# A grouped 3x3 convolution: from two 64x128 TensorE tiles per tap to eight 32x64 tiles

## The chip, the cores and the metric

The kernel runs on one core of a Trainium2 chip. The metric is the device time of one execution in microseconds (us). Of the kernel before there are three runs: 154.03, 154.77 and 154.79 us, median 154.77 us. Lower is better.

## The reference

A 2-D convolution with a 3x3 kernel, padding 1 and 8 groups, on 16 images of 64x64 pixels. 64 input channels become 128 output channels; a group is 8 input channels and 16 output channels.

```python
batch, c_in, h, w, c_out, k, groups = 16, 64, 64, 64, 128, 3, 8
x_pad = np.pad(x, ((0, 0), (0, 0), (pad, pad), (pad, pad)), mode='constant')
# for each group g, image b, output channel co, input channel ci of the group, tap (kh, kw):
output[b, g * c_out_per_group + co] += \
    weight[g * c_out_per_group + co, ci, kh, kw] * \
    x_pad[b, g * c_in_per_group + ci, kh:kh+h, kw:kw+w]
```

x and the output are float32: 16.8 MB are read and 33.6 MB written. The arithmetic on TensorE is in bf16 with float32 sums.

## The kernel before

**Layout.** Two images of 64 channels fill the 128 partitions. An image lies in SBUF as one flat row of 4096 bf16 pixels per channel, with 66 zeros ahead of it and behind it (`PADL`, `PADR`). Eight such pairs make the batch (`NPAIR`). The loads are cast from float32 to bf16 on the way, and are issued from Pool's queue (lines 106 and 118); the first pair is loaded image by image into two buffers, `xpa` and `xpb`, so that its work can start early.

**Taps as shifts.** A tap (kh, kw) is a shift of the flat row by `W*(kh-1) + (kw-1)`. For each chunk of 512 pixels (8 rows) the loop at line 162 issues nine taps, each with two matmuls at line 170: one on the upper 64 rows of the array for the first image, one on the lower 64 rows for the second. Each has 64 input channels by all 128 output channels, with the weights of the other groups as zeros, and accumulates in a PSUM bank of its own (`pcs[h]`).

**Edges.** A flat shift runs over the ends of image rows: the taps with kw = 0 and kw = 2 add, in the first and last column, pixels of the neighbouring row. What they add too much is computed separately: VectorE gathers the two border columns into `xc` (lines 128 to 131), twelve small matmuls a pair (line 149) multiply them into `fxa` and `fxb`, and VectorE subtracts these from the output tile (lines 213 and 218).

**Copies and stores.** Each bank is copied to the output tile `ob` by ScalarE (line 195) or VectorE (line 197), in turns. Stores go out on Pool's queue (line 223), half an image at a time, in the last pair a quarter.

**Weights.** They are loaded on the sync queue (line 48, `w_sb`), transposed by a matmul with an identity (line 51), expanded to block form by nine float32 matmuls with selection matrices (line 84) and masked by VectorE into `wtap` (line 88). Pool builds the selection matrices and the mask with selects (lines 58, 72, 76).

**What sets the order.** The framework orders each engine's instructions by readiness and by their place in the program, and puts in the semaphores. Each engine's queue then runs in that order. Buffers: six for input, six for output, two PSUM banks for each of `pc0` and `pc1`.

Of the kernel before, what the change touches and what calls it, by code (L numbers as in the profile page):

```python
# [8 lines left out]
FP32 = mybir.dt.float32  # L10
BF16 = mybir.dt.bfloat16


@with_exitstack
def kernel(
# [7 lines left out]
    nc = tc.nc  # L23

    B, C, H, W = x.shape
    CO, CIg, K, _ = weight.shape
    G = groups
    COg = CO // G
    HW = H * W
    assert C == 64 and CO == 128 and K == 3 and B % 2 == 0  # L30

    PADL = W + 2
    PADR = W + 2
    XBUF = PADL + HW + PADR

    wpool = ctx.enter_context(tc.tile_pool(name="wpool", bufs=1))
    xpool = ctx.enter_context(tc.tile_pool(name="xpool", bufs=6))
    opool = ctx.enter_context(tc.tile_pool(name="opool", bufs=6))
    colpool = ctx.enter_context(tc.tile_pool(name="colpool", bufs=3))
    psum_o = ctx.enter_context(tc.tile_pool(name="psum_o", bufs=2, space=bass.MemoryType.PSUM))  # L40
    psum_f = ctx.enter_context(tc.tile_pool(name="psum_f", bufs=2, space=bass.MemoryType.PSUM))

    ident = wpool.tile([128, 128], FP32)
    make_identity(nc, ident)

    w_sb = wpool.tile([128, CIg * K * K], FP32)
    with tc.high_priority(offset=100000):
        nc.sync.dma_start(w_sb, weight.rearrange("co ci kh kw -> co (ci kh kw)"))

    wT_ps = psum_f.tile([128, 128], FP32, tag="fixA", name="wT_ps")  # L50
    nc.tensor.transpose(wT_ps[0 : CIg * K * K, :], w_sb, ident)  # L51
    wT = wpool.tile([128, 128], FP32)
    nc.vector.tensor_copy(wT[0 : CIg * K * K, :], wT_ps[0 : CIg * K * K, :])  # L53

    sel = wpool.tile([128, 9, 128], FP32)
    nc.vector.memset(sel, 0.0)
    for t in range(9):
        nc.gpsimd.affine_select(  # L58
            out=sel[:, t, :],
            in_=sel[:, t, :],  # L60
            compare_op=mybir.AluOpType.not_equal,
            fill=1.0,
            base=-t,
            channel_multiplier=1,
            pattern=[[0, 2], [0, G], [-9, CIg]],
        )

    maskBD = wpool.tile([128, 128], FP32)
    nc.vector.memset(maskBD, 0.0)
    for h in range(2):  # L70
        msl = maskBD[64 * h : 64 * h + 64, :]
        nc.gpsimd.affine_select(
            out=msl, in_=msl, compare_op=mybir.AluOpType.is_gt, fill=1.0,
            base=1 - CIg, channel_multiplier=1, pattern=[[-CIg, G], [0, COg]],
        )
        nc.gpsimd.affine_select(  # L76
            out=msl, in_=msl, compare_op=mybir.AluOpType.is_ge, fill=0.0,
            base=0, channel_multiplier=1, pattern=[[-CIg, G], [0, COg]],
        )

    wtap = wpool.tile([128, 9, 128], BF16)
    for t in range(9):
        U = psum_f.tile([128, 128], FP32, tag="fixA", name=f"U{t}")
        nc.tensor.matmul(  # L84
            U, lhsT=sel[0 : CIg * K * K, t, :], rhs=wT[0 : CIg * K * K, :],
            start=True, stop=True,
        )
        nc.vector.tensor_mul(wtap[:, t, :], U, maskBD)  # L88

    x_pairs = x.rearrange("b c h w -> (b c) (h w)").rearrange(  # L90
        "(i p) s -> i p s", p=128
    )
    out3 = out.rearrange("b co h w -> b co (h w)")

    NPAIR = B // 2
    NCHUNK = HW // 512
    xps = {}

    def emit_load(i):
        if i == 0:  # L100
            xpa = xpool.tile([128, XBUF], BF16, name="xpa", tag="xpa", bufs=1)
            xpb = xpool.tile([128, XBUF], BF16, name="xpb", tag="xpb", bufs=1)
            for h, t_ in enumerate((xpa, xpb)):
                nc.vector.memset(t_[64 * h : 64 * h + 64, 0:PADL], 0.0)
                nc.vector.memset(t_[64 * h : 64 * h + 64, PADL + HW :], 0.0)
                nc.gpsimd.dma_start(
                    t_[64 * h : 64 * h + 64, PADL : PADL + HW],
                    x_pairs[0][64 * h : 64 * h + 64, :],
                )
            xps[i] = (xpa, xpb)  # L110
            return
        xp = xpool.tile([128, XBUF], BF16, name="xp")
        nc.vector.memset(xp[:, 0:PADL], 0.0)
        nc.vector.memset(xp[:, PADL + HW :], 0.0)
        npiece = 2 if i == 1 else 1
        ppc = HW // npiece
        for pp in range(npiece):
            nc.gpsimd.dma_start(  # L118
                xp[:, PADL + ppc * pp : PADL + ppc * (pp + 1)],
                x_pairs[i][:, ppc * pp : ppc * (pp + 1)],  # L120
            )
        xps[i] = (xp, xp)

    emit_load(0)
    emit_load(1)

    def emit_gather(xp, xc):
        nc.vector.memset(xc, 0.0)
        xp3 = xp[:, PADL : PADL + HW].rearrange("p (h w) -> p h w", w=W)
        nc.vector.tensor_copy(xc[:, 2 : 2 + H], xp3[:, :, W - 1])  # L130
        nc.vector.tensor_copy(xc[:, 72 : 72 + H], xp3[:, :, 0])

    for i in range(NPAIR):
        if i + 2 < NPAIR:
            emit_load(i + 2)
        xph = xps.pop(i)

        fixs = [
            psum_f.tile([128, 2, H], FP32, tag="fixA", name="fxa"),
            psum_f.tile([128, 2, H], FP32, tag="fixB", name="fxb"),  # L140
        ]
        xc = colpool.tile([128, 152], BF16, name="xc")

        def emit_fix_group(g):
            h, e = g // 2, g % 2
            pr = 64 * h
            off = 0 if e == 0 else 72
            for kh in range(3):
                nc.tensor.matmul(  # L149
                    fixs[h][:, e, :],  # L150
                    wtap[pr : pr + 64, 3 * kh + 2 * e, :],
                    xc[pr : pr + 64, off + kh : off + kh + H],
                    start=(kh == 0), stop=(kh == 2), tile_position=(pr, 0),
                )

        fix_c0 = 3 if i < 2 else 0

        ob = [
            opool.tile([128, HW], FP32, name=f"ob{h}_{i}", tag="ob") for h in range(2)
        ]  # L160

        for c in range(NCHUNK):
            pcs = [psum_o.tile([128, 512], FP32, name=f"pc{h}") for h in range(2)]
            for t in range(9):
                kh, kw = t // 3, t % 3
                d = W * (kh - 1) + (kw - 1)
                base = PADL + 512 * c + d
                for h in range(2):
                    pr = 64 * h
                    nc.tensor.matmul(  # L170
                        pcs[h],
                        wtap[pr : pr + 64, t, :],
                        xph[h][pr : pr + 64, base : base + 512],
                        start=(t == 0), stop=(t == 8), tile_position=(pr, 0),
                    )
            if c == fix_c0:
                if i > 0:
                    emit_gather(xph[0], xc)
                else:
                    for h in range(2):  # L180
                        xp3 = xph[h][64 * h : 64 * h + 64, PADL : PADL + HW]
                        xp3 = xp3.rearrange("p (h w) -> p h w", w=W)
                        nc.vector.memset(xc[64 * h : 64 * h + 64, :], 0.0)
                        nc.vector.tensor_copy(  # L184
                            xc[64 * h : 64 * h + 64, 2 : 2 + H], xp3[:, :, W - 1]
                        )
                        nc.vector.tensor_copy(  # L187
                            xc[64 * h : 64 * h + 64, 72 : 72 + H], xp3[:, :, 0]
                        )
            if fix_c0 <= c < fix_c0 + 4:  # L190
                emit_fix_group(c - fix_c0)
            for h in range(2):
                dst = ob[h][:, 512 * c : 512 * (c + 1)]
                if (c + h) % 2 == 0:
                    nc.scalar.copy(dst, pcs[h])  # L195
                else:
                    nc.vector.tensor_copy(dst, pcs[h])  # L197

            if c == 0:
                stored = 0  # L200
            last_pair = i == NPAIR - 1
            qn = 4 if last_pair else 2
            qc = NCHUNK // qn
            if c >= fix_c0 + 3:
                ready_q = (c + 1) // qc
                while stored < ready_q:
                    q = stored
                    stored += 1
                    r0 = q * (H // qn)
                    s0 = r0 * W  # L210
# [51 lines left out]
```

## Time and profile before

| What | Value |
|---|---|
| median of the three runs | 154.77 us |
| span of the profiled execution, first to last instruction | 152.7 us |
| busy share: TensorE, its weight loads | 90%, 59% |
| busy share: VectorE, ScalarE, Pool | 41%, 25%, 20% |
| mean rate of the DMA | 276 GB/s |
| read from and written to HBM | 16.81 MB, 33.55 MB |

The span is that of one execution under the profiler; the run times are those of whole executions, so the median lies 2.1 us above the span. In the page, PE is TensorE's matmuls, PEld its weight loads, DVE VectorE, ACT ScalarE, POOL GpSimd and SP SyncE. Two rows cut the span into 40 slices of 3.8 us: one with the busy share in tenths, one with the rate in GB/s. The DMA's rate counts bytes where they land, so a load that is cast from float32 to bf16 counts with half of what it reads. In the groups of instructions, a row gives the line, engine, operation, operands, shapes and count, then busy us and mean ns of one, then the engine's idle time before them and what ended it.

### The profile page before, as it was taken

How to read it: one execution, taken by the hardware profiler on the slowest of the kernel's cores; microseconds unless marked ns; L12 is line 12 of the kernel's file. 1: busy time of each engine (PE TensorE's matmuls, PEld its weight loads, DVE VectorE, ACT ScalarE, POOL GpSimd, SP SyncE). 2: the span in 40 equal slices, each digit the busy share in tenths (PEclk: the TensorE clock that was granted, in tenths of full speed). 3: DMA queues.
4: the chain of work that ended last, by engine and by line, in shares of the span. 5: the costliest groups of instructions: out<-in, count | busy, mean ns of one | idle time of the engine just before them, and what ended most of it. 6: DMA issues, size and time to landing. Idle time of an engine off the chain costs nothing.

```text
span 152.7 us, 3024 instructions
## 1 busy us (share of the span) xinstructions
PE 137.4 (90%) x1267; PEld 90.7 (59%) x1267; DVE 62.0 (41%) x193; ACT 38.8 (25%) x65; POOL 29.8 (20%) x65
## 2 busy tenths in 40 slices
PE   1199999999999999999999999999999999999700
PEld 0155344577766667766776667766776677667400
DVE  6132153454334535353535353434353535454400
ACT  3000113322222333333333333222223333333300
POOL 7990000112011402020202020201101020214220
PEclk9999999999999999999999999999999999999965
DMA  3489999999999999999994929394948576696961
GB/s 63 84 149 207 228 210 219 217 213 219 159 419 427 419 404 210 369 416 434 423 416 208 414 107 412 137 378 178 369 180 339 217 309 245 275 406 260 374 276 63
DMA packets 6654, 42.18 MB, mean 276 GB/s; under 512 B 880, under 2 KB 880, under 8 KB 2160
## 3 DMA queue, kind: packets, MB, share of 16 engines
q0 software_dynamic: 6496, 41.95, 81.3%
q8 instruction: 10, 0.16, 0.4%
q1 hardware_dynamic: 144, 0.04, 0.1%
q14 instruction: 4, 0.03, 0.1%
HBM read 16.81 MB, written 33.55 MB: 330 GB/s over the span
## 4 chain that ended last, share of the span: by engine, by line
PE 89%; DMA 3%; issue 2%; POOL 0%; DVE 0%; POOLq 0%; DVEq 0%
PE pc L170 84%; PE U L84 4%; DMA xpa<-in_x_dram 3%; PE fxa L149 1%; PE fxb L149 1%; POOLq L257 0%; POOL out_dram L223 0%; DVE xc L187 0%; POOL ident masks.py:197 0%; DVE xc L184 0%; DVE wT L53 0%; POOLq L223 0%; POOLq masks.py:199 0%; DVEq L184 0%; POOLq L243 0%
## 5 line engine op out<-in xcount | busy, mean ns | idle before, releaser
L170 PE MATMUL pc<-xp,wtap 64*128 64x512 bf16 x1008 | 110.8, 376 | 0.0
L170 PEld LDWEIGHTS <-wtap 64*128 64x128 bf16 x1152 | 85.2, 94 | 38.0 <-issue 3.7
L197 DVE COPY ob<-pc 128x512 f32<-128x512 f32 x64 | 44.3, 692 | 72.1 <-PE pc L170 72.1
L195 ACT COPY ob<-pc 128x512 f32<-128x512 f32 x64 | 37.5, 586 | 105.2 <-PE pc L170 104.1
L223 POOL DMA_DIRECT2D out_dram<-ob x36 | 19.1, 532 | 115.3 <-DVE ob L218 86.9
L170 PE MATMUL pc<-xpa,wtap 64*128 64x512 bf16 x72 | 19.9, 423 | 0.0
L170 PE MATMUL pc<-xpb,wtap 64*128 64x512 bf16 x72 | 18.0, 411 | 0.0
L149 PEld LDWEIGHTS <-wtap 64*128 64x128 bf16 x96 | 6.8, 93 | 5.5
L84 PE MATMUL U<-wT,sel 72*128 72x128 f32 x18 | 5.6, 464 | 4.0 <-DVE wT L53 3.9
L84 PEld LDWEIGHTS U<-wT,sel 72*128 72x128 f32 x18 | 4.2, 320 | 6.6 <-POOL maskBD L76 4.2
L88 DVE TENSOR_TENSOR wtap<-U,maskBD 128x128 bf16<-128x128 f32 x9 | 2.6, 292 | 5.8 <-PE U L84 5.3
L118 POOL DMA_DIRECT2D xp<-in_x_dram x8 | 4.3, 542 | 0.3 <-PE pc L170 0.3
L213 DVE TENSOR_TENSOR ob<-ob,fxa 128x32 f32<-128x32 f32 (+1 forms) x18 | 3.6, 203 | 1.3
L149 PE MATMUL fxb<-xc,wtap 64*128 64x64 bf16 x48 | 4.0, 190 | 0.0
L149 PE MATMUL fxa<-xc,wtap 64*128 64x64 bf16 x48 | 4.0, 190 | 0.0
L213 DVE TENSOR_TENSOR ob<-ob,fxb 128x32 f32<-128x32 f32 (+1 forms) x18 | 3.5, 194 | 0.0
L218 DVE TENSOR_TENSOR ob<-ob,fxa 128x32 f32<-128x32 f32 (+1 forms) x18 | 3.5, 194 | 0.0
L218 DVE TENSOR_TENSOR ob<-ob,fxb 128x32 f32<-128x32 f32 (+1 forms) x18 | 3.5, 192 | 0.0
L58 POOL TENSOR_SCALAR_AFFINE_SELECT sel<-sel 128x128 f32<-128x128 f32 x9 | 3.2, 399 | 0.0
L51 PE MATMUL wT_ps<-ident,w_sb 128*72 128x128 f32 x1 | 0.4, 397 | 2.8 <-POOL sel L58 2.8
L51 PEld LDWEIGHTS wT_ps<-ident,w_sb 128*72 128x72 f32 x1 | 0.1, 136 | 2.8 <-POOL sel L58 2.8
L130 DVE COPY xc<-xp 128x64 bf16<-128x64 bf16 x7 | 1.5, 215 | 0.1
(27 smaller groups left out, 11.4 us busy)
## 6 DMA issues: line engine op xcount, KB each, us to landing
out_dram<-ob POOLq DMA_DIRECT2D x28, 1024.0 KB, 7.6
xp<-in_x_dram POOLq DMA_DIRECT2D x6, 1024.0 KB, 20.1
out_dram<-ob POOLq DMA_DIRECT2D x8, 512.0 KB, 4.4
xp<-in_x_dram POOLq DMA_DIRECT2D x2, 512.0 KB, 7.8
xpa<-in_x_dram POOLq DMA_DIRECT2D x1, 512.0 KB, 4.9
xpb<-in_x_dram POOLq DMA_DIRECT2D x1, 512.0 KB, 4.8
w_sb<-in_weight_dram SPq DMA_DIRECT2D x1, 36.0 KB, 1.9
```

What stands on the lines that cost most here:

```text
L58: nc.gpsimd.affine_select(out=sel[:, t, :], in_=sel[:, t, :], compare_op=mybir.AluOpType.not_equal, fill=1.0, base=-t, channel_multiplier= ...
L84: nc.tensor.matmul(U, lhsT=sel[0 : CIg * K * K, t, :], rhs=wT[0 : CIg * K * K, :], start=True, stop=True,)
L88: nc.vector.tensor_mul(wtap[:, t, :], U, maskBD)
L118: nc.gpsimd.dma_start(xp[:, PADL + ppc * pp : PADL + ppc * (pp + 1)], x_pairs[i][:, ppc * pp : ppc * (pp + 1)],)
L130: nc.vector.tensor_copy(xc[:, 2 : 2 + H], xp3[:, :, W - 1])
L149: nc.tensor.matmul(fixs[h][:, e, :], wtap[pr : pr + 64, 3 * kh + 2 * e, :], xc[pr : pr + 64, off + kh : off + kh + H], start=(kh == 0), st ...
L170: nc.tensor.matmul(pcs[h], wtap[pr : pr + 64, t, :], xph[h][pr : pr + 64, base : base + 512], start=(t == 0), stop=(t == 8), tile_position ...
L195: nc.scalar.copy(dst, pcs[h])
L197: nc.vector.tensor_copy(dst, pcs[h])
L213: nc.vector.tensor_sub(ov[:, r0 : r0 + H // qn, 0], ov[:, r0 : r0 + H // qn, 0], fixs[h][:, 0, r0 : r0 + H // qn],)
L218: nc.vector.tensor_sub(ov[:, r0 : r0 + H // qn, W - 1], ov[:, r0 : r0 + H // qn, W - 1], fixs[h][:, 1, r0 : r0 + H // qn],)
L223: nc.gpsimd.dma_start(out3[2 * i + h][:, s0 : s0 + HW // qn], ob[h][:, s0 : s0 + HW // qn],)
```

## The change

The convolution is cut into eight tiles of the array, 32 rows (4 groups in) by 64 columns (4 groups out), and the edge correction goes.

- **Two layouts of the input, all of it resident.** Images 0 to 7 lie in four tensors `xn`, two images each. Images 8 to 15 lie in four tensors `xs`, moved by 32 rows (half an image), so that the half images of both layouts together fall on all eight pairs of a row quarter and a column half. Each image is loaded once. All loads stand at the start of the program, on Pool's queue: nine pieces for the first pair of tensors, four for each of the other three, 21 in all.
- **Streams.** A step `i` works on four images (2i, 2i+1, 8+2i, 9+2i) with eight streams, a half image each; a chunk of 8 rows takes nine taps times eight matmuls.
- **Clipped taps.** The input has no padding; each tap reads and writes only those pixels for which its shifted source exists. The centre tap comes first. The edge matmuls, gathers and subtractions go.
- **Weights.** VectorE spreads them and masks them to block form `E` (five multiplications); 18 bf16 matmuls with an identity transpose them into `wN` and `wS` (two copies of the weights in two row orders). Pool builds mask and identity by three selects, which stand behind the loads in the program.
- **Copies and stores.** Copies out of PSUM as before, four a chunk, in turns on ScalarE and VectorE. Output tiles hold half an image; there are 16. Stores of 1 MB go out on the sync queue, four after every fourth chunk. PSUM has eight banks of one kind (`ps`), two sets of four.

The core of the diff:

```diff
-    xpool = ctx.enter_context(tc.tile_pool(name="xpool", bufs=6))
-    opool = ctx.enter_context(tc.tile_pool(name="opool", bufs=6))
-    psum_o = ctx.enter_context(tc.tile_pool(name="psum_o", bufs=2, space=bass.MemoryType.PSUM))
+    xpool = ctx.enter_context(tc.tile_pool(name="xpool", bufs=1))
+    opool = ctx.enter_context(tc.tile_pool(name="opool", bufs=16))
+    psum = ctx.enter_context(tc.tile_pool(name="psum", bufs=8, space=bass.MemoryType.PSUM))
+    xr = x.rearrange("b c h w -> (b c) (h w)")
+    xn = [xpool.tile([128, H, W], BF16, name=f"xn{i}") for i in range(4)]
+    xs = [xpool.tile([128, H, W], BF16, name=f"xs{i}") for i in range(4)]
...
+    def load(t, row0, p0, p1, h0, h1):
+        nc.gpsimd.dma_start(
+            flat(t)[p0:p1, h0 * W : h1 * W],
+            xr[row0 + p0 : row0 + p1, h0 * W : h1 * W],
         )
...
+    nc.sync.dma_start(w_sb, weight.rearrange("co ci kh kw -> co (ci kh kw)"))
+    cuts = [0, 16, 32, 64]
+    for h0, h1 in zip(cuts, cuts[1:]):
+        load(xn[0], 0, 0, 128, h0, h1)
+        load(xs[3], 512 - 96, 96, 128, h0, h1)
+        load(xs[0], 544, 0, 128, h0, h1)
+    for i in range(1, 4):
+        for h0, h1 in ((0, 32), (32, 64)):
+            load(xn[i], 128 * i, 0, 128, h0, h1)
+            load(xs[i], 544 + 128 * i, 0, 128 if i < 3 else 96, h0, h1)
...
+    nc.gpsimd.affine_select(
+        out=mask, in_=mask, compare_op=ALU.is_ge, fill=0.0,
...
+    nc.gpsimd.affine_select(
+        out=ident, in_=ident, compare_op=ALU.not_equal, fill=1.0,
...
+    for r in range(5):
+        g0 = 4 * (r % 2)
+        nc.vector.tensor_mul(
+            E[:, :, 32 * r : 32 * r + 32].rearrange("p t (g c) -> p t g c", c=CIg),
+            wv.unsqueeze(2).to_broadcast([128, T, 4, CIg]),
+            mask[:, g0 : g0 + 4].unsqueeze(1).unsqueeze(3).to_broadcast([128, T, 4, CIg]),
         )
...
+    for k, (wt, off) in enumerate(((wN, 0), (wS, 32))):
+        for t0 in range(0, T, 4):
...
+                nc.tensor.matmul(
+                    ps[:, 128 * t : 128 * t + 128],
+                    E[:, t0 + t, off : off + 128],
+                    ident,
+                    start=True, stop=True,
+                )
...
+    def mm(dst, wt, xt, q, half, c, kh, kw, first, last):
+        lo, hi = max(0, R * c + kh - 1), min(H, R * c + R + kh - 1)
+        o0 = lo - (R * c + kh - 1)
+        w0, w1 = max(0, kw - 1), min(W, W + kw - 1)
+        v0 = w0 - (kw - 1)
+        nr, nw = hi - lo, w1 - w0
+        d3 = dst.rearrange("p (h w) -> p h w", w=W)
+        nc.tensor.matmul(
+            d3[64 * half : 64 * half + 64, o0 : o0 + nr, v0 : v0 + nw],
+            wt[32 * q : 32 * q + 32, 3 * kh + kw, 64 * half : 64 * half + 64],
+            xt[32 * q : 32 * q + 32, lo:hi, w0:w1],
+            start=first, stop=last,
+            tile_position=(32 * q, 64 * half),
         )
...
+        streams = [
+            (0, wN, xn[i], 0, 0), (2, wS, xs[i], 0, 1),
+            (0, wN, xn[i], 1, 1), (3, wS, xs[i], 1, 0),
+            (1, wN, xn[i], 2, 0), (3, wS, xs[i], 2, 1),
+            (1, wN, xn[i], 3, 1), (2, wS, prev, 3, 0),
         ]
...
+            for k, (kh, kw) in enumerate(taps):
+                for b, wt, xt, q, half in streams:
+                    mm(pcs[b], wt, xt, q, half, c, kh, kw, k == 0, k == T - 1)
+            for b in range(4):
+                dst = obs[b][:, 512 * (c % 4) : 512 * (c % 4) + 512]
+                if nev % 2 == 0:
+                    nc.scalar.copy(dst, pcs[b])
                 else:
+                    nc.vector.tensor_copy(dst, pcs[b])
+                nev += 1
+            if c % 4 == 3:
+                s0 = HALF * (c // 4)
+                for b in range(4):
+                    nc.sync.dma_start(outf[imgs[b]][:, s0 : s0 + HALF], obs[b])
```

In `streams` a stream is: which of the four images, the weights, the input tensor, the row quarter q and the column half.

More of the change, by code (lines that the diff above doesn't have):

```diff
@@ L6 @@
 from concourse import bass_utils, mybir
-from concourse.masks import make_identity
 from concourse._compat import with_exitstack
@@ L11 @@
 BF16 = mybir.dt.bfloat16
+ALU = mybir.AluOpType
 @with_exitstack
@@ L29 @@
     HW = H * W
[L30 to L34, printed above, removed]
-    wpool = ctx.enter_context(tc.tile_pool(name="wpool", bufs=1))
-    xpool = ctx.enter_context(tc.tile_pool(name="xpool", bufs=6))
-    opool = ctx.enter_context(tc.tile_pool(name="opool", bufs=6))
-    colpool = ctx.enter_context(tc.tile_pool(name="colpool", bufs=3))
-    psum_o = ctx.enter_context(tc.tile_pool(name="psum_o", bufs=2, space=bass.MemoryType.PSUM))
@@ L41 @@
[L41 to L65, printed above, removed]
-        )
-    maskBD = wpool.tile([128, 128], FP32)
@@ L69 @@
[L69 to L74, printed above, removed]
-        )
-        nc.gpsimd.affine_select(
-            out=msl, in_=msl, compare_op=mybir.AluOpType.is_ge, fill=0.0,
-            base=0, channel_multiplier=1, pattern=[[-CIg, G], [0, COg]],
-        )
@@ L81 @@
[L81 to L140, printed above, removed]
-        ]
[L142 to L178, printed above, removed]
-                else:
[L180 to L210, printed above, removed]
-                    for h in range(2):
-                        ov = ob[h].rearrange("p (r w) -> p r w", w=W)
-                        nc.vector.tensor_sub(
-                            ov[:, r0 : r0 + H // qn, 0],
-                            ov[:, r0 : r0 + H // qn, 0],
-                            fixs[h][:, 0, r0 : r0 + H // qn],
-                        )
-                        nc.vector.tensor_sub(
-                            ov[:, r0 : r0 + H // qn, W - 1],
-                            ov[:, r0 : r0 + H // qn, W - 1],
-                            fixs[h][:, 1, r0 : r0 + H // qn],
-                        )
-                        nc.gpsimd.dma_start(
-                            out3[2 * i + h][:, s0 : s0 + HW // qn],
-                            ob[h][:, s0 : s0 + HW // qn],
-                        )
@@ new lines @@
+    T = K * K
+    assert (B, C, CO, K, G, H, W) == (16, 64, 128, 3, 8, 64, 64)
+    R = 8
+    NCH = H // R
+    HALF = HW // 2
+    wpool = ctx.enter_context(tc.tile_pool(name="wpool", bufs=1))
+    xpool = ctx.enter_context(tc.tile_pool(name="xpool", bufs=1))
[3 more added lines that the diff above has]
+    xn = [xpool.tile([128, H, W], BF16, name=f"xn{i}") for i in range(4)]
@@ new lines, with flat @@
+    xs = [xpool.tile([128, H, W], BF16, name=f"xs{i}") for i in range(4)]
+    def flat(t):
+        return t.rearrange("p h w -> p (h w)")
+    def load(t, row0, p0, p1, h0, h1):
+        nc.gpsimd.dma_start(
+            flat(t)[p0:p1, h0 * W : h1 * W],
+            xr[row0 + p0 : row0 + p1, h0 * W : h1 * W],
+        )
+    w_sb = wpool.tile([128, CIg * T], FP32)
+    nc.sync.dma_start(w_sb, weight.rearrange("co ci kh kw -> co (ci kh kw)"))
[4 more added lines that the diff above has]
+        load(xs[0], 544, 0, 128, h0, h1)
@@ new lines @@
+    for i in range(1, 4):
+        for h0, h1 in ((0, 32), (32, 64)):
+            load(xn[i], 128 * i, 0, 128, h0, h1)
+            load(xs[i], 544 + 128 * i, 0, 128 if i < 3 else 96, h0, h1)
+    mask = wpool.tile([128, G], FP32)
+    nc.vector.memset(mask, 1.0)
+    nc.gpsimd.affine_select(
+        out=mask, in_=mask, compare_op=ALU.is_ge, fill=0.0,
+        base=0, channel_multiplier=1, pattern=[[-COg, G]],
+    )
+    nc.gpsimd.affine_select(
+        out=mask, in_=mask, compare_op=ALU.is_ge, fill=0.0,
+        base=COg - 1, channel_multiplier=-1, pattern=[[COg, G]],
+    )
@@ new lines @@
+    ident = wpool.tile([128, 128], BF16)
+    nc.vector.memset(ident, 0.0)
+    nc.gpsimd.affine_select(
+        out=ident, in_=ident, compare_op=ALU.not_equal, fill=1.0,
+        base=0, channel_multiplier=1, pattern=[[-1, 128]],
+    )
+    E = wpool.tile([128, T, 160], BF16)
+    wv = w_sb.rearrange("co (ci t) -> co t ci", t=T)
+    ge = 160 // CIg
+    for r in range(5):
[4 more added lines that the diff above has]
+            mask[:, g0 : g0 + 4].unsqueeze(1).unsqueeze(3).to_broadcast([128, T, 4, CIg]),
+        )
@@ new lines @@
+    wN = wpool.tile([128, T, 128], BF16)
+    wS = wpool.tile([128, T, 128], BF16)
+    for k, (wt, off) in enumerate(((wN, 0), (wS, 32))):
+        for t0 in range(0, T, 4):
+            n = min(4, T - t0)
+            ps = psum.tile([128, 512], FP32, name="ps", tag="ps")
+            for t in range(n):
+                nc.tensor.matmul(
[3 more added lines that the diff above has]
+                    start=True, stop=True,
+                )
+            dst = wt[:, t0 : t0 + n, :].rearrange("p t c -> p (t c)")
+            if k == 0:
+                nc.vector.tensor_copy(dst, ps[:, 0 : 128 * n])
+            else:
+                nc.scalar.copy(dst, ps[:, 0 : 128 * n])
@@ new lines @@
+    outf = out.rearrange("b co h w -> b co (h w)")
+    taps = [(1, 1)] + [(a, b) for a in range(3) for b in range(3) if (a, b) != (1, 1)]
+    def mm(dst, wt, xt, q, half, c, kh, kw, first, last):
[11 more added lines that the diff above has]
+            tile_position=(32 * q, 64 * half),
+        )
@@ new lines @@
+    nev = 0
+    for i in range(4):
+        imgs = [2 * i, 2 * i + 1, 8 + 2 * i, 9 + 2 * i]
+        prev = xs[i - 1]
+        streams = [
[3 more added lines that the diff above has]
+            (1, wN, xn[i], 3, 1), (2, wS, prev, 3, 0),
+        ]
+        obs = None
+        for c in range(NCH):
+            if c % 4 == 0:
+                obs = [opool.tile([128, HALF], FP32, name=f"ob{i}_{c}_{b}", tag="ob") for b in range(4)]
+            pcs = [psum.tile([128, 512], FP32, name="ps", tag="ps") for b in range(4)]
+            for k, (kh, kw) in enumerate(taps):
[5 more added lines that the diff above has]
+                    nc.scalar.copy(dst, pcs[b])
+                else:
+                    nc.vector.tensor_copy(dst, pcs[b])
[4 more added lines that the diff above has]
+                    nc.sync.dma_start(outf[imgs[b]][:, s0 : s0 + HALF], obs[b])
```

## The prediction

> **What bounds the kernel now.** I read the page first, for busy shares and for the chain that ended last.
>
> ```profile
> span 152.7 us, 3024 instructions
> PE 137.4 (90%) x1267; PEld 90.7 (59%) x1267; DVE 62.0 (41%) x193; ACT 38.8 (25%) x65; POOL 29.8 (20%) x65
> ...
> DMA  3489999999999999999994929394948576696961
> GB/s 63 84 149 207 228 210 219 217 213 219 159 419 427 419 404 210 369 416 434 423 416 208 414 107 412 137 378 178 369 180 339 217 309 245 275 406 260 374 276 63
> ...
> HBM read 16.81 MB, written 33.55 MB: 330 GB/s over the span
> ...
> PE 89%; DMA 3%; issue 2%; POOL 0%; DVE 0%; POOLq 0%; DVEq 0%
> ```
>
> TensorE holds the chain for 89% of the span. But the DMA row is at 9 in slices 5 to 22 and falls to 4 to 8 only afterwards: transfers are the second limit, not far below. So I need two paces, TensorE's and the DMA's. TensorE's pace comes from the chain (start, length, what) and from the timeline (start, length, instruction).
>
> ```profile
> 15.07 10.03 PE pc L170 x59
> ...
> 57.62 9.48 PE pc L170 x87
> ...
> 73.38 9.48 PE pc L170 x87
> ```
> ```profile
> 19.23 0.63 PE L170 MATMUL pc<-xpb,wtap 64*128 64x512 bf16 x1
> ...
> 19.66 0.63 PE L170 MATMUL pc<-xpb,wtap 64*128 64x512 bf16 x1
> ...
> 20.57 0.38 PE L170 MATMUL pc<-xpb,wtap 64*128 64x512 bf16 x1
> ...
> 20.79 0.38 PE L170 MATMUL pc<-xpb,wtap 64*128 64x512 bf16 x1
> ```
>
> One pair of images takes 73.38 - 57.62 = 15.76 us for 72 rounds (8 chunks, 9 taps), each of two matmuls on two row tiles. Two matmuls on the same row tile start 0.22 us apart (0.216 when 15.76 us are shared over 72 rounds and a little goes to the 12 edge matmuls). Both tiles keep that pace, so the two run side by side and their weight loads are hidden. Before 20 us the same step took 0.43 us: dense work begins at 15.07, and the array ran at half speed for its first 5 us, although the clock row of the page shows nothing of it. Eight pairs need 8 x 15.76 = 126 us: this is the bound.
>
> The DMA's pace comes from two stretches in the windows view, one with loads alone and one with stores alone, in which the DMA share is full.
>
> ```profile
> core 0: us, PE busy (x) PEld busy (x) DVE busy (x) ACT busy (x) POOL busy (x), PEclk, DMA share, GB/s
> 17.00:38.00 21.00, 21.00 (x187) 11.52 (x185) 8.66 (x25) 5.38 (x10) 2.14 (x4) 1.00 1.03 215
> 42.00:57.30 15.30, 15.30 (x160) 10.04 (x157) 6.58 (x21) 4.41 (x8) 2.67 (x5) 1.00 1.03 416
> ```
>
> Loads are counted in bf16 as they land, so 215 GB/s is 430 GB/s of float32 read. The kernel reads 16.81 MB (8.39 MB landed) and writes 33.55 MB: 8.39/0.215 = 39.0 us plus 33.55/0.416 = 80.7 us, 119.7 us in all. TensorE's 126 us stands only 6 us above that floor.
>
> **The convolution.** The change replaces 1152 matmuls (64 rows by 128 columns, of whose weights one in eight is not zero) and 96 edge matmuls by 32 chunks x 9 taps x 8 tiles = 2304 matmuls of 32 by 64. In rounds of eight there are 288. If a round costs what a round costs now, TensorE needs 288 x 0.216 = 62.2 us. Clipped taps stream 504 columns instead of 512; I give no credit for that. Whether eight go side by side, with eight weight loads in each round, the trace does not show; it shows two. The nearest rows are a burst in which short edge matmuls (fxb) mix with long ones.
>
> ```profile
> 57.37 0.19 PE L149 MATMUL fxb<-xc,wtap 64*128 64x64 bf16 x1
> 57.37 0.09 PEld L149 LDWEIGHTS <-wtap 64*128 64x128 bf16 x1
> ...
> 57.38 0.09 PEld L170 LDWEIGHTS <-wtap 64*128 64x128 bf16 x1
> 57.39 0.38 PE L170 MATMUL pc<-xp,wtap 64*128 64x512 bf16 x1
> 57.40 0.19 PE L149 MATMUL fxb<-xc,wtap 64*128 64x64 bf16 x1
> 57.40 0.09 PEld L149 LDWEIGHTS <-wtap 64*128 64x128 bf16 x1
> 57.41 0.09 PEld L170 LDWEIGHTS <-wtap 64*128 64x128 bf16 x1
> ```
>
> Three matmuls and four loads start within 0.04 us, about 6 ns each; 16 instructions a round would need some 100 ns, below 216. Loads that start 10 ns apart each last 90 ns, so on two row tiles they overlap. The other end is loads one at a time: 2304 x 94 ns = 217 us (mean in the rows below). I take 216 ns a round, by the burst, which is the nearer row, and keep the other end for the rivals.
>
> **Copies out of PSUM.** Same count and shape, four a chunk.
>
> ```profile
> L170 PEld LDWEIGHTS <-wtap 64*128 64x128 bf16 x1152 | 85.2, 94 | 38.0 <-issue 3.7
> L197 DVE COPY ob<-pc 128x512 f32<-128x512 f32 x64 | 44.3, 692 | 72.1 <-PE pc L170 72.1
> L195 ACT COPY ob<-pc 128x512 f32<-128x512 f32 x64 | 37.5, 586 | 105.2 <-PE pc L170 104.1
> ...
> L88 DVE TENSOR_TENSOR wtap<-U,maskBD 128x128 bf16<-128x128 f32 x9 | 2.6, 292 | 5.8 <-PE U L84 5.3
> ...
> L58 POOL TENSOR_SCALAR_AFFINE_SELECT sel<-sel 128x128 f32<-128x128 f32 x9 | 3.2, 399 | 0.0
> ```
>
> VectorE's two cost 2 x 0.692 = 1.38 us, under a chunk's 9 x 0.216 = 1.94 us; with two sets of four banks they hide behind the next chunk. That cover is gone only below 154 ns a round. VectorE's edge subtractions, gathers and memsets go too; they lay beside matmuls, so nothing is gained.
>
> **Loads, Pool's queue and the weights.** The x bytes are unchanged (each image is loaded once, into one of the two layouts), but all 21 loads now stand first in Pool's program order, ahead of the three selects from which the masks and the identity come, and so ahead of all weights.
>
> ```profile
> 1.36 0.65 POOL L106 DMA_DIRECT2D xpa<-in_x_dram  x1 [0.34 <-issue]
> ...
> 7.68 3.74 POOL L118 DMA_DIRECT2D xp<-in_x_dram  x7
> ```
> ```profile
> out_dram<-ob POOLq DMA_DIRECT2D x28, 1024.0 KB, 7.6
> ...
> out_dram<-ob POOLq DMA_DIRECT2D x8, 512.0 KB, 4.4
> ...
> xpa<-in_x_dram POOLq DMA_DIRECT2D x1, 512.0 KB, 4.9
> ...
> w_sb<-in_weight_dram SPq DMA_DIRECT2D x1, 36.0 KB, 1.9
> ```
>
> An issue costs 3.74/7 = 0.53 us, so 21 end at 1.4 + 11.2 = 12.6 us at the earliest. Here never more than about eight transfers were outstanding on this queue. If each load must wait for the one eight before it, the last waits for load 13, at 8.9 of 16.8 MB: 1.4 + 2.5 + 8.9/0.43 = 24.6 us. (2.5 us is fixed: xpa took 4.9 us for 0.52 MB, which at 215 GB/s are 2.4.) After that come three selects (0.4 us at most, 1.0 in all), five multiplications of 288 elements (between 0.29 for 128 and 0.69 for 512, say 0.45, 2.2 in all), eight short transposes (some 0.1 us each, 0.8) and two copies of 0.69 (1.4): an estimate of 5.4 us. The first convolution matmul starts at 18 or at 30 us. I take 30, by the count of eight.
>
> The half-speed start costs another 2.6 us (5 us at half pace). The first batch of stores (four chunks, 36 rounds) is then ready at 30 + 2.6 + 36 x 0.216 + 0.7 = 41 us. The last load lands at 1.4 + 2.5 + 39.0 = 42.9 us. So the late weights cost almost nothing: the DMA is busy with loads until then. That is the cover; every microsecond later than about 31 us would be lost.
>
> **Stores.** 32 stores of 1 MB on the sync queue instead of 36 on Pool's. Only the 36 KB of w_sb used that queue; its 1.9 us are no price for 1 MB. I bound the rate by 427 GB/s (best slice) and by 10% less than 416; I take 416, since the same memories and engines move it. In SP's queue nothing stands behind a waiting store but later stores. A half batch makes 4.19 MB, which the DMA needs 10.1 us for, while TensorE makes it in 7.8: from here the DMA is the bound, and buffers for four batches let TensorE run ahead.
>
> **The sum.** The last store lands at 42.9 + 80.7 = 123.6 us, up to 1 us later for the gap between loads and stores. The end now: the last store was issued at
>
> ```profile
> 145.65 1.07 POOL L223 DMA_DIRECT2D out_dram<-ob  x2 [2.83 <-DVE ob L218]
> ```
>
> so at 146.2, landed 4.4 us later at 150.6, and the span ended 2.1 us after that. Span 123.6 + 2.1 = 125.7, up to 126.7. The median run is 154.77 us for a span of 152.7, so 2.1 us lie outside. That gives 127.8 to 128.8; I say 128.0 us.
>
> **The rivals.** If TensorE and not the DMA sets the end, the time for a round of R ns is 30 + 2.6 + 288R + 0.7, then the last batch (2.5 + 10.1), the end (2.1) and what lies outside (2.1): 50.1 us + 288R. The DMA stays the bound up to R = 270 ns; the old time is reached at 363 ns.
>
> First, slower: rounds split in two. Each PSUM tile is now written by two row tiles, on its upper and lower partitions, while in the kernel before each row tile has a bank of its own, so that no row shows a shared bank. If such pairs go one after the other, a round costs 2 x 216 = 432 ns and the time is 174 us (162 with the early weights). Against it: partitions differ, and instructions of different tiles start 10 ns apart here. [...]
>
> Second, slower: weight loads go one by one. Half of 94 ns for half the columns is 47 ns, eight make 376 ns a round: 158 us, or 146 with the early weights. Against it speaks the burst. [...]
>
> Third, in between: rounds of 290 to 360 ns, from output rows of 63 elements with odd starts, of which the kernel before has none, or from 16 instructions a round. At 320 ns: 142 us.
>
> Fourth, the DMA is slower than in the stretches above, because two queues mix or the sync queue's stores run 10% lower: 80.7 becomes 89.7 us, the time 137 us.
>
> **How the numbers follow.** Forecast (124 to 132 us) 0.60; fourth 0.10; third 0.12; first 0.12; second 0.06. About 0.5% (154.0 to 155.5 us) is what a measurement can tell from no change. The third at its upper edge (0.02) and the second between its two starts (0.01) come near that: 0.03. The first and the rest of the second are slower, 0.17. What remains, 0.60 + 0.10 + 0.10, is faster, 0.80. The range runs from 123 us (best rates 427 and 219 GB/s take off 2.8 us, overlap of fixed parts 2 more) to 148 us, which takes in the fourth and most of the third and leaves out the slower 0.17 and some 0.03 at the edges.
>
> **What would show it.** Right: matmuls of one tile start 0.22 us apart with eight in flight; DMA at 9 from slice 2 to the end; loads done near 42 us, first stores near 41; TensorE idle for a third of the span, waiting late for ob; the chain ends in DMA. Wrong: a PE that is never idle after its start with rounds above 270 ns, a load stretch or store stretch clearly below 215 and 416 GB/s, or a gap between the two because the weights come after 31 us.

## The result and the profile after

The changed kernel takes 148.43 us (median of four runs) against 154.52 us (median of four). Two of its four runs, 150.38 and 150.58 us, and one run further below (140.95 us, selects first with rows of 2 KB) came out slow, 1.5% or more above the fastest of the same kernel, and are left out of all ratios. The other two, 146.28 and 146.47 us, give a ratio of 0.947 to the kernel before, 95% interval 0.944 to 0.951. The forecast was 128.0 us, in a range of 123 to 148. The 146.28 and 146.47 us lie just inside the upper edge of that range, but what holds them there is not what the forecast rests on.

The page of the changed kernel (144.5 us of span in a run of 146.28 us):

```profile
span 144.5 us, 4928 instructions
...
PE   0000000049966954769792993899549499930000
...
DMA  3999999999997996995199799749999925998991
GB/s 41 118 185 214 215 215 210 213 214 217 215 206 219 426 426 277 413 410 245 75 428 413 290 426 413 295 168 401 426 426 422 415 91 211 404 426 367 428 424 75
...
q1 hardware_dynamic: 4752, 33.59, 56.0%
q0 software_dynamic: 2672, 8.39, 30.4%
q8 instruction: 18, 0.29, 0.8%
...
PE 53%; issue 17%; DMA 16%; DVE 2%; POOL 2%; DVEq 0%; POOLq 0%
```

The loads come at 215 GB/s and the stores at 400 to 428, as forecast. But the DMA row has holes from slice 13 on, where it should read 9 to the end, and TensorE's row has holes too. The chain gives 17% to "issue": time in which the engine waited for nothing that the profile shows. Before it was 2%. The chain in order of time (start, length, what) shows where that is:

```profile
32.87 7.82 PE ps L131 x142
40.69 1.22 issue
41.91 3.66 PE ps L131 x128
45.57 1.44 issue
47.01 3.66 PE ps L131 x128
...
55.94 2.64 issue
58.58 5.29 PE ps L131 x128
...
69.60 7.12 PE ps L131 x256
...
103.20 3.46 issue
106.66 5.29 PE ps L131 x128
111.96 2.00 issue
113.96 12.26 PE ps L131 x384
...
130.34 0.68 DVE ob L163
```

The convolution runs from 32.87 to 130.34 us: 97.5 us, where the forecast had 62.2 and 2.6 for the half-speed start. The rows named issue are TensorE's stops. They come after 128 matmuls, or 256, or 384 (a number slightly below is one with missing records); that is not the period of the loop, whose chunk has 72 matmuls. With each matmul goes a weight load, so 128 matmuls are 256 instructions. The instruction queue q8 moved 0.29 MB in 18 packets, 16 KB each, or 64 bytes for each of 256 instructions. In the trace such a packet ends 1.2 to 1.6 us before the end of each of the twelve stops. So the theory to test is A: TensorE has used up its instructions and waits for the next block. Its rival is B: TensorE waits for PSUM banks or output tiles that copies and stores hold.

### The profile page after: what moved, and what is told of

Same layout as the page of the kernel before. It is cut to its first block, busy times and chain, and to the rows that moved or that the text cites. A ratio compares the mean times of both kernels' runs of the same rounds, so it can differ in the third digit from the quotient of the medians.

```text
span 144.5 us, 4928 instructions
## 1 busy us (share of the span) xinstructions
PE 77.0 (53%) x2322; PEld 51.5 (36%) x2322; DVE 45.7 (32%) x74; ACT 37.1 (26%) x68; POOL 12.0 (8%) x28
## 3 DMA queue, kind: packets, MB, share of 16 engines
q0 software_dynamic: 2672, 8.39, 30.4%
## 4 chain that ended last, share of the span: by engine, by line
PE 53%; issue 17%; DMA 16%; DVE 2%; POOL 2%; DVEq 0%; POOLq 0%
PE ps L131 52%; DMA xs<-in_x_dram 11%; DMA xn<-in_x_dram 5%; DVE E L94 2%; PE ps L107 1%; POOL xn L53 1%; POOL xs L53 1%; DVE ob L163 0%; DVEq L199 0%; POOL ident L85 0%; POOL mask L75 0%; POOLq L199 0%; POOLq L75 0%; POOLq L185 0%
## 5 line engine op out<-in xcount | busy, mean ns | idle before, releaser
L131 PE MATMUL ps<-xs,wS 32*64 32x504 bf16 (+3 forms) x1152 | 73.7, 412 | 22.6 <-issue 22.4
L131 PE MATMUL ps<-xn,wN 32*64 32x504 bf16 (+3 forms) x1152 | 74.9, 413 | 0.0
L163 DVE COPY ob<-ps 128x512 f32<-128x512 f32 x64 | 41.2, 686 | 57.5 <-PE ps L131 57.5
L131 PEld LDWEIGHTS <-wS 32*64 32x64 bf16 x1152 | 47.3, 115 | 18.6 <-issue 3.1
L161 ACT COPY ob<-ps 128x512 f32<-128x512 f32 x64 | 34.6, 589 | 63.1 <-PE ps L131 54.3
L131 PEld LDWEIGHTS <-wN 32*64 32x64 bf16 x1152 | 40.3, 115 | 29.1 <-issue 27.8
L107 PE MATMUL ps<-ident,E 128*128 128x128 bf16 x18 | 2.1, 313 | 30.8 <-DVE E L94 30.8
L94 DVE TENSOR_TENSOR E<-w_sb,mask 128x288 bf16<-128x288 f32 x5 | 2.9, 643 | 27.4 <-POOL mask L79 27.4
L53 POOL DMA_DIRECT2D xs<-in_x_dram x12 | 6.4, 536 | 9.9 <-DMA xs<-in_x_dram 7.3
L53 POOL DMA_DIRECT2D xn<-in_x_dram x9 | 5.0, 550 | 6.0 <-DMA xn<-in_x_dram 4.6
## 6 DMA issues: line engine op xcount, KB each, us to landing
xs<-in_x_dram POOLq DMA_DIRECT2D x1, 128.0 KB, 9.5
```

Of the source, the lines that this page charges most:

```text
L53: nc.gpsimd.dma_start(flat(t)[p0:p1, h0 * W : h1 * W], xr[row0 + p0 : row0 + p1, h0 * W : h1 * W],)
L94: nc.vector.tensor_mul(E[:, :, 32 * r : 32 * r + 32].rearrange("p t (g c) -> p t g c", c=CIg), wv.unsqueeze(2).to_broadcast([128, T, 4, CIg]),
L107: nc.tensor.matmul(ps[:, 128 * t : 128 * t + 128], E[:, t0 + t, off : off + 128], ident, start=True, stop=True,)
L131: nc.tensor.matmul(d3[64 * half : 64 * half + 64, o0 : o0 + nr, v0 : v0 + nw], wt[32 * q : 32 * q + 32, 3 * kh + kw, 64 * half : 64 * half ...
L161: nc.scalar.copy(dst, pcs[b])
L163: nc.vector.tensor_copy(dst, pcs[b])
```

## The experiments

Times are medians of four runs; the stores of few bytes and the additional instructions were run once. The kernel before, run beside each, took 154.1 to 154.5 us.

**The selects ahead of the loads.** The block of loads is moved behind the three selects:

```diff
-    cuts = [0, 16, 32, 64]
-    for h0, h1 in zip(cuts, cuts[1:]):
-        load(xn[0], 0, 0, 128, h0, h1)
...
     nc.gpsimd.affine_select(
         out=ident, in_=ident, compare_op=ALU.not_equal, fill=1.0,
         base=0, channel_multiplier=1, pattern=[[-1, 128]],
     )
+    cuts = [0, 16, 32, 64]
+    for h0, h1 in zip(cuts, cuts[1:]):
+        load(xn[0], 0, 0, 128, h0, h1)
...
```

> Theory A (TensorE stops for its instructions: they come in blocks of 256, 128 weight loads and 128 matmuls, and a block is asked for only when the one before it begins, so it arrives 3 us later when the DMA is quiet and up to 6 us later when it is busy, against the 3.5 us in which eight tiles use a block up): TensorE, not the DMA, sets the end, so its start counts. With the three selects ahead of the loads the first convolution matmul starts near 11 us instead of 32.8; the convolution still takes some 97 us, the last half batch of stores 13 us: 125 to 133 us instead of 146. The step on record (the late weights are hidden behind the loads, the DMA sets the end): no change, 145 to 147 us.

Measured: 133.17 us, ratio 0.861 (0.856 to 0.865). The late weights were not hidden: moving them is worth 13 us. The time lies at the upper edge of what was expected, but the convolution does not: it starts at 7.1 us instead of 11 and takes 109.0 us instead of 97, with 30.0 us of stops. The page's DMA rows are now nearly full:

```profile
span 131.4 us, 4928 instructions
...
DMA  1899999999999999999999999999999999969970
GB/s 29 112 163 196 216 217 207 312 302 326 318 311 317 314 308 324 307 317 321 312 342 415 427 412 422 427 427 412 424 427 409 397 414 424 427 262 419 427 329 10
...
q1 hardware_dynamic: 4752, 33.59, 61.8%
q0 software_dynamic: 2672, 8.39, 33.5%
```

The shares of the two queues give 95.3% of 131.4 = 125.2 us of DMA work; in the changed kernel it was 86.4% of 144.5 = 124.8 us. The work is the same, and nearly all the holes have gone.

**Stores of few bytes.** Most of the output is left out: only 64 of 2048 columns of each tile are stored.

```diff
-                    nc.sync.dma_start(outf[imgs[b]][:, s0 : s0 + HALF], obs[b])
+                    nc.sync.dma_start(outf[imgs[b]][:, s0 : s0 + 64], obs[b][:, 0:64])
```

> Leaves out most of the output: each store writes 64 of its 2048 columns, all else as before. Theory A with the DMA as the cause of the late blocks: after the loads the DMA is quiet, a block arrives in some 3.3 us, and the stops all but vanish: convolution 97.5 us falls to 65 to 72, span near 110 us. If blocks are slow whatever the DMA does: stops stay, convolution 95 us or more. Theory B (stops are waits for output tiles or PSUM banks that stores hold): vanish as well, so this run does not part A from B.

Measured: 108.51 us, span 106.5 us. The convolution takes 70.6 us, within the 65 to 72 that were expected. From the chain in order of time:

```profile
47.25 7.01 PE ps L131 x247
54.26 0.44 issue
54.70 14.03 PE ps L131 x512
68.73 0.33 issue
```

As soon as the loads are done (46 us), the DMA is quiet (share 0.08 from 60 to 90 us) and the stops shrink to 0.44 us and less: a block comes over the DMA, and arrives nearly in time when the DMA is quiet. The row of 512 matmuls gives the pace of eight tiles without stops: 14.03 us for 64 rounds, 0.219 us a round.

**More instructions.** One additional weight load for every second matmul; the arithmetic stays the same.

```diff
+                    if half == 0:
+                        nc.tensor.ldweights(
+                            wt[32 * q : 32 * q + 32, 3 * kh + kw, 0:64],
+                            tile_position=(32 * q, 0),
+                        )
                     mm(pcs[b], wt, xt, q, half, c, kh, kw, k == 0, k == T - 1)
```

> Every second matmul gets one more weight load of the same weights, which changes no result: 20 instructions a round instead of 16, about 23 blocks instead of 18. Theory A: a block lasts 2.8 us instead of 3.5 and still takes 3 to 6 us to arrive: five more stops and longer ones, convolution 115 to 125 us, time 163 to 175. Theory B (waits for output tiles or banks): stores, copies and tiles are the same, so 146 us, 3 at most above.

Measured: 163.23 us. From the chain in order of time:

```profile
65.67 3.60 PE ps L131 x103
69.28 2.60 issue
71.88 12.18 PE ps L131 x305
84.06 1.47 issue
```

The stops have moved: they now come after 102 or 103 matmuls or a multiple (305), and 256 instructions at 2.5 a matmul are 102.4 matmuls. Instruction packets are 22 instead of 18. Chunks, copies, banks and stores are as in the changed kernel, so B, under which the stops would have stayed where they were, falls.

The time does not decide between the two, although it lies in the range expected of A. A block of 103 takes 3.60 us where 128 took 3.66, that is 0.28 us a round instead of 0.229: the four additional weight loads of a round are not free. Over 288 rounds that makes 14.6 us of the 16.9 us by which the convolution is longer (114.4 us instead of 97.5), while the stops add up to 23.2 us, hardly more than the 22.6 of the changed kernel. The 2.8 us expected of such a block came too low, and longer stops did not come. In the trace the first seven or so rounds behind the stop at 84.06 us start 0.216 us apart, and from then on a round takes 0.290 us. No run shows what sets the 0.290 us.

**Smaller stores.** After each chunk, in rows of 2 KB, and then after every second chunk, in rows of 4 KB, with the selects where the change has them:

```diff
-            if c % 4 == 3:
-                s0 = HALF * (c // 4)
-                for b in range(4):
-                    nc.sync.dma_start(outf[imgs[b]][:, s0 : s0 + HALF], obs[b])
+            s0 = 512 * c
+            for b in range(4):
+                nc.sync.dma_start(
+                    outf[imgs[b]][:, s0 : s0 + 512],
+                    obs[b][:, 512 * (c % 4) : 512 * (c % 4) + 512],
+                )
```

> Stores after each chunk, 128 of 256 KB (rows of 2 KB) instead of 32 of 1 MB (rows of 8 KB). Theory A: the last stores carry 1 MB instead of 4.2 MB, 7.6 us less at 416 GB/s: 139 us; up to 10 us better still if a block of instructions waits behind single rows in the DMA, since these are four times shorter. Theory B: the same 7.6 us and tiles come free a little sooner. Against both: if rows of 2 KB lower the rate by over a tenth, no gain.

Measured: 142.79 us, ratio 0.923 (0.918 to 0.929); the convolution takes 83.5 us instead of 97.5. The time came out 4 us above the 139 expected.

> The changed kernel with rows of 4 KB, stores after every second chunk, selects where they are. If a block of instructions waits behind single rows in the DMA, the stops lie between those of rows of 8 KB (convolution 97.5 us) and of 2 KB (83.5 us): 88 to 93 us, and the time 140 to 144 us. If only the earlier start of the stores shortened them, as short as with 2 KB rows or as long as with 8 KB.

Measured: 139.49 us, ratio 0.904 (0.900 to 0.908), with 93.7 us of convolution. Both are faster than the changed kernel, and the convolution lies between the other two, a little above the 88 to 93 expected, with a time half a microsecond below. Alone that would fit the idea that a block waits behind single rows. The next two runs speak against it.

**Both together.** Selects first, with stores after each chunk or after every second one:

> Selects ahead of the loads and stores after each chunk in rows of 2 KB. Theory A: TensorE starts near 11 us and its stops are the shorter ones, so it is done by 100 us and the DMA sets the end at last: 3.9 + 39.0 us of loads, 33.55 MB at the 400 GB/s of such rows (83.9 us), 2.1 at the end and 2.1 outside: 129 to 132 us. If the two gains were the same gain (both only fill the DMA's gaps), no better than 133.

Measured: 139.76 us, ratio 0.904 (0.898 to 0.910).

> As before, with stores after every second chunk, rows of 4 KB. Theory A: the DMA is the bound at 410 to 416 GB/s (81.3 us) with a tail of 2.1 MB: 128 to 131 us.

Measured: 135.38 us, ratio 0.879 (0.873 to 0.885). Both missed, and both are slower than the selects alone. Their queue shares say why, first of the 2 KB and then of the 4 KB rows:

```profile
span 137.7 us, 5119 instructions
...
q1 hardware_dynamic: 18576, 33.60, 65.0%
q0 software_dynamic: 2672, 8.39, 31.7%
```
```profile
span 133.1 us, 5000 instructions
...
q1 hardware_dynamic: 9360, 33.60, 63.2%
q0 software_dynamic: 2672, 8.39, 33.1%
```

The DMA's work is 96.7% of 137.7 = 133.2 us and 96.3% of 133.1 = 128.2 us, against 125.2 with rows of 8 KB: smaller rows cost DMA time. The DMA is the bound there, since the convolution ends at 102.2 and 114.0 us and the DMA goes on at 9 tenths for more than 10 us, and its work accounts for the difference (6.3 us of span and 8 of work for 2 KB, 1.7 and 3.0 for 4 KB). I had taken 83.9 us for the stores; 65.0% of 137.7 are 89.5. As to the stops, first 4 KB rows and then 2 KB rows, from the chain:

```profile
70.93 5.33 PE ps L129 x128
76.25 0.59 issue
76.85 3.66 PE ps L129 x128
80.51 2.26 issue
82.77 3.56 PE ps L129 x119
86.33 2.37 issue
```
```profile
56.81 2.26 issue
59.06 3.50 PE ps L129 x114
62.57 2.42 issue
...
87.08 0.94 issue
88.02 3.66 PE ps L129 x128
91.68 0.34 issue
```
```profile
core 0: us, PE busy (x) PEld busy (x) DVE busy (x) ACT busy (x) POOL busy (x), PEclk, DMA share, GB/s
56.00:68.00 12.00, 7.32 (x224) 4.64 (x216) 3.87 (x6) 3.22 (x6) 0.00 (x0) 0.88 1.05 401
84.00:100.00 16.00, 14.06 (x503) 9.62 (x481) 8.60 (x14) 7.22 (x15) 0.00 (x0) 1.00 0.93 346
```

With the DMA full (share 1.05 in the windows of the 2 KB kernel) a stop lasts 2.3 to 2.4 us with rows of 2 KB too; with the DMA a little below full (0.93) it lasts 0.3 to 0.9 us. It is how full the queues are that sets the stop, and not the size of a row. In the full stretches the packet of a block starts 3.6 to 4.0 us after TensorE went on with the block before, takes 0.9 us, and TensorE goes on some 1.4 us after it: 6 us, of which 3.7 are hidden behind the block before. With a quiet DMA (the stores of few bytes) the first of these three is near 1.1 us. In the changed kernel it is 4.0 us from 58.58 us on, at a DMA share of 1.03, and 1.1 us from 69.60 us on, at 0.05; its 18 packets start 0.25 to 4.89 us after TensorE took up the block before, none ahead of that. When a block is asked for, no record shows. How a packet waits within the queues was not separated further.

The first rows (4 KB) show that these 6 us, and not TensorE's pace, sets the time in a full stretch. The block from 70.93 us ran at a lower clock (0.71 granted from there to 76.85 us, 5.33 us of matmuls instead of 3.66), and the stop behind it was shorter by as much: 5.33 + 0.59 and 3.66 + 2.26 us both make 5.92.

**What is left.** With the selects ahead of the loads, the last half batch is stored in two parts, first alone and then with larger load pieces (the change of `cuts`):

```diff
-    cuts = [0, 16, 32, 64]
+    cuts = [0, 32, 64]
...
-            if c % 4 == 3:
+            n = 2 if (i == 3 and c >= 4) else 4
+            if c % n == n - 1:
...
```

> e1_selects_first with the last half batch stored in two parts, nothing else: 1 to 2 us of the DMA's idle stretch ahead of the last batch go, 131 to 132.5 us. Beside it e8_fewer_pieces shows what the load pieces cost.

> Selects ahead of the loads, the first loads in two pieces instead of three (rows of 32 lines, no row under 4 KB landed), and the last half batch stored in two parts. Theory A with the DMA as the last bound: the 576 short load packets of e1_selects_first took 0.22 us each for 2 KB against 0.32 for 4 KB, so 2 us go; the idle stretch of the DMA ahead of the last batch shrinks by 1 to 2 us: 130 us, between 129 and 132. If TensorE and its stops still set the end, 133 as with the selects alone.

Measured: 133.32 us, ratio 0.865 (0.861 to 0.868), for the split alone, and 132.48 us, ratio 0.858 (0.854 to 0.862), with the larger pieces too. Both expectations were missed by about half a microsecond or more. The split brings nothing over the selects alone (0.861), although the DMA row has no hole ahead of the last batch any more; why not was not followed up. The larger pieces bring 0.8 us beside it, less than the 2 us that I had reckoned, and as much as the loads' work falls (33.7% of 131.0 = 44.1 us, then 33.1% of 130.7 = 43.3); this last version is the fastest of all, but its interval overlaps with that of the selects alone.

## Why the prediction was wrong

The step that failed is "16 instructions a round would need some 100 ns, below 216". It priced instructions by a burst of seven that were already at hand (0.04 us), and took a pace from it that must hold for 4644 of them (2322 weight loads and 2322 matmuls). The pace of eight tiles itself was right: 0.219 us a round against 0.216. What was not asked is how fast instructions arrive. A block of 256 lasts 14 us at the old pace (128 matmuls at 0.109 us), so its 6 us never showed; at the new pace it lasts 3.7 us and they do. The kernel before could have told half of that. Its page has q8 in the section on queues, and 16 KB of instructions by eight tiles in 3.5 us is a number that I could have worked out; the 6 us it does not show.

```profile
q0 software_dynamic: 6496, 41.95, 81.3%
q8 instruction: 10, 0.16, 0.4%
```

Point by point:

- **The convolution.** Forecast 64.8 us with the half-speed start, measured 97.5. The 288 rounds at 0.219 us are 63.1 us of that. The stops in the chain add up to 22.6 us. The array also falls back to half speed: 5.29 us for 128 matmuls instead of 3.66, at a granted clock of 0.68, after the stops of 2.64 and 3.46 us (behind the second one the clock is 0.50 from 108.1 to 111.0 us, and a round takes 0.43 us). It happens five times, after all stops of 2.00 us and more but the last, at some 1.6 us each time: 8 us. The remaining 3.8 us are the half-speed start (some 2 us) and the ends of the blocks (a block before a stop takes 3.66 us, one without a stop 14.03/4 = 3.51). The length of a stop does not alone decide on the half speed: with the selects first, a block behind a stop of 2.64 us took 3.61 us. Nor is its price simply added: by the rows with a full DMA above, a slower block shortens the stop behind it.
- **Start of the convolution.** Forecast 30 us by the count of eight outstanding loads, measured 32.87. The count was right (in the trace never more than eight loads are outstanding), and the selects had to wait for the last load's issue, which came at 27.2 us instead of 24.6.
- **"The late weights cost almost nothing."** Wrong as a consequence: that held only while the DMA set the end. With TensorE behind, its start counts until the DMA takes over: by the run with the selects first, a start 25.7 us earlier gave 13 us, since the fuller DMA made the convolution 11.5 us longer.
- **The DMA.** Rates as forecast (215, and 400 to 428), also on the sync queue, so the fourth rival falls as far as the rate goes. The loads ended some 3 us later than 42.9 us, at 45.8. By the queue shares the stores took 56.0% of 144.5 = 80.9 us, as forecast (80.7), and the loads 30.4%, 43.9 us instead of 39.0. The changed kernel has no more DMA work than the one before: there q0, which has nearly all the transfers, had 81.3% of 152.7 = 124.1 us. The forecast took 39.0 us from the rate of one steady stretch; in the second and third slices the DMA is at 9 tenths with 118 and 185 GB/s.
- **The end.** The formula for the case in which TensorE sets the end, 50.1 us + 288R, gives 147.6 us for 97.5 us, of which 2.6 are counted twice, and 2.8 more for the later start: 147.8, against 146.3.
- **The rivals.** The time came out near the third one's, 142 us at 320 ns, since the average round was 97.5/288 = 339 ns, but by another mechanism. It named "16 instructions a round" as one of two reasons, but as a longer round and not as stops between blocks. Odd rows of 63 elements cost nothing that shows in 0.219 us. The first rival, banks shared by two row tiles, falls with the same number: 432 ns a round would have shown. The second falls as well: a load of 64 columns takes 115 ns where one of 128 took 94, but loads run side by side (1152 of 115 ns are 132 us, in 47.3 us of busy time; the eight of the round at 65.91 us start within 0.05 us and last 0.105 us each):

```profile
L131 PEld LDWEIGHTS <-wS 32*64 32x64 bf16 x1152 | 47.3, 115 | 18.6 <-issue 3.1
```

With the selects moved, the DMA does what was forecast of it: it is full almost from start to end, at 132.5 to 133.3 us. TensorE does not, since it still stops for its instructions. The 5 us that remain to the forecast are as much as the term for the loads was too small: 33.5% of 131.4 = 44.0 us instead of 39.0.

## What to carry to other kernels

An engine that is made several times faster by smaller tiles must also be fed several times faster with instructions: divide 256 instructions by the new rate, and compare that with the 6 us that a block took to arrive here while the DMA was full (some 3.4 us while it was quiet). A preparation step that is hidden behind a transfer is hidden only as long as that transfer sets the end, so put it ahead of a long list of loads whenever that is free. Where a profile says "issue", count the instructions between two stops: a constant count that ignores the loop's own period points to the supply of instructions.

## What the hardware showed beside that

- Eight tiles of 32 by 64, with outputs that share banks by partition halves and rows of 63 elements, run at 0.219 us a round of 504 or 512 columns; the two tiles of before took 0.216 for 512.
- A packet of 16 KB with instructions takes 0.9 us (0.88 to 0.97 us for 15 of the 18 in the changed kernel, 1.7 at most), and TensorE goes on some 1.4 us after it ends (1.2 to 1.6 us at the twelve stops). The packet starts 1.1 us after TensorE took up the block before in a quiet DMA (share 0.05), and 3.6 to 4.0 us after it in a full one; in the changed kernel the longest are 4.6 and 4.9 us (shares 1.02 and 1.01).
- Two queues with work share the DMA: in the run with the selects first, loads and stores together moved 302 to 326 GB/s as they land, between 215 for loads alone and 420 for stores alone, with a full share (1.04 from 20 to 45 us).
